# Attention in a two-layer hybrid backbone: transposing all key blocks of two heads, then multiplying both groups' values in one stretch

## The chip, the cores and the metric

The kernel runs on one core of a Trainium2 chip. The metric is device time in microseconds, the median of 3 runs: 1319.07 us (1317.4 to 1320.59). The profile is of one execution of its own.

## The reference, cut to what matters

Two layers, each with three head groups beside each other: a Hyena long convolution, a Mamba-2 scan and windowed attention. 512 latent tokens and 256 context tokens, model width 1024. The change touches attention alone: 8 query heads of 64 channels in 2 groups of 4 that share a key and value head. A latent block of 128 queries sees its own and its neighbouring key blocks and both context blocks; a context block sees the context blocks.

```python
s_loc = jnp.einsum("bnqhgd,bnkhd->bnhgqk", qb, kband).astype(jnp.float32) * scale
s_loc = jnp.where(mask[None, :, None, None], s_loc, -jnp.inf)
s_ctx = jnp.einsum("bnqhgd,bkhd->bnhgqk", qb, kc).astype(jnp.float32) * scale
sink = jnp.broadcast_to(sinks..., (b, nb, ATT_KV_HEADS, ATT_GROUP, WINDOW, 1))
p = jax.nn.softmax(jnp.concatenate([s_loc, s_ctx, sink], -1), axis=-1).astype(v.dtype)
o = (jnp.einsum("bnhgqk,bnkhd->bnqhgd", p[..., :nloc], vband)
     + jnp.einsum("bnhgqk,bkhd->bnqhgd", p[..., nloc:nloc + lc], vc))
```

Everything is float32. The context's own output is needed in layer 0 only.

## The kernel before, in words

`att` (from L577) works through blocks of 128 queries: n = 0 to 3 of the latent tokens and, in layer 0, n = 4 and 5 of the context. A block has nk key blocks of 128: 4, 5, 5, 4 for the latent ones and 2, 2 for the context's. That is 22 key blocks in layer 0 and 18 in layer 1, 40 in all.

For each of the two groups g the block's queries are loaded (L599), split in a high and a low part (`qh`, `ql`), multiplied with the keys (L614, L622, L630, masks L631) and put through a softmax (maxima L632 and L633, exponentials L634 and L636, scaling by the reciprocal sum L645 on ACT for head 3 and L647 on DVE for heads 0 to 2). The probabilities of a group are one tile `pr`, with the queries on the partitions; both groups' tiles are kept in `prs`.

For the product with the values the keys have to be on the partitions. So for each key block i and each group g, four transposes (L654, one a head) fill a bank of PSUM (`wk`, five banks), and a copy brings it to a tile `pt` in SBUF (five buffers of 128 x 512): on DVE (L659), or on ACT (L657) where g is 1 and i is not 0. Then one product a group (L663) adds the block to the accumulator `pv`, which is a bank of `wk` too: group 0 writes partitions 0 to 63, group 1 partitions 64 to 127, 512 columns (four heads) each. A float32 product is two records in the trace. At the end of a block of queries ACT takes the accumulator out (L664) and SP stores it (L665).

The order of the instructions on each engine is not the order of the program text. The tile framework draws it up at compile time: it takes what is ready by its own model of times, in the priority of the program's order, subject to data, free buffers and explicit edges of order; on the chip each engine then keeps that order. This is how the projections of the other head groups (`proj`: L450 for the latent tokens, L452 for the context's) get in among the attention work.

Of the kernel before, what the change touches and what calls it, by code (L numbers as in the profile page):

```python
# [35 lines left out]
# columns of the per-layer parameter block  # L36
C_HCW, C_SCW, C_NW, C_BM = 0, 48, 80, 84
NPAR = 108
# columns of the constant block
K_ID, K_U, K_L, K_ONE = 0, 128, 256, 384  # L40
NCON = 512
# blocks of 128 columns of w_in
# [3 lines left out]
class Net:  # L46
    def __init__(self, ctx, tc, a):
        self.tc, self.nc, self.a = tc, tc.nc, a
        nc = self.nc
        self.one = ctx.enter_context(tc.tile_pool(name="one", bufs=1))  # L50
        self.dr = ctx.enter_context(tc.tile_pool(name="dr", bufs=1, space=DRAM))
        self.ps = ctx.enter_context(tc.tile_pool(name="ps", bufs=1, space=PSUM))
        self.sb = ctx.enter_context(tc.tile_pool(name="sb", bufs=1))
        self.n = 0
        self.kd = {}
        self.th = {}
        self.ph = None
        self.rr = 0

        self.ml = self.tq([P, 4, 768])  # L60
        fw = self.ml[:, 3]
        self.fw = fw
        nc.sync.dma_start(self.ml.rearrange("p a b -> p (a b)")[0:33, 1536:2432], a["mlp1"])
        self.cc = self.one.tile([P, 16], F32, name="cc")
        nc.sync.dma_start(self.cc, a["cc"])
        nc.sync.dma_start(fw[:, 128:392], a["mlp2"])
        self.row = self.one.tile([P, DEPTH, 48], F32, name="row")
        nc.sync.dma_start(self.row, a["row"].partition_broadcast(P))
        self.con = self.one.tile([P, NCON], F32, name="con")
        nc.sync.dma_start(self.con, a["con"])  # L70
        self.ident = self.con[:, K_ID:K_ID + P]
        self.par = self.one.tile([P, DEPTH, NPAR], F32, name="par")
        nc.sync.dma_start(self.par, a["par"].rearrange("l p n -> p l n"))
        self.identb = self.one.tile([P, P], BF16, name="identb")
        nc.vector.tensor_copy(self.identb, self.ident)
        self.maskb = self.one.tile([P, 2, P], BF16, name="maskb")
        mk = self.ip("V", [P, QW])[:, :2 * P]
        nc.sync.dma_start(mk, a["mask"])
        nc.vector.tensor_copy(self.maskb.rearrange("p a b -> p (a b)"), mk)
        self.upper = self.one.tile([P, P], mybir.dt.uint8, name="upper")  # L80
        nc.vector.tensor_copy(self.upper, self.con[:, K_U:K_U + P])
        gc = self.one.tile([P, 512], F32, name="gc")
        self.gc = gc.rearrange("p (q s k) -> p q s k", q=2, s=2)
        self.mhalf = self.one.tile([P, 16], F32, name="mhalf")
        nc.vector.memset(self.mhalf, -0.5)
        for l in range(DEPTH):
            s = self.par[:, l, C_SCW:C_SCW + 32]
            nc.vector.tensor_scalar_mul(s, s, 0.5)
        self.nega = self.one.tile([P, DEPTH, 16], F32, name="nega")
        self.nsink = self.one.tile([P, DEPTH, 8], F32, name="nsink")  # L90
        nc.vector.tensor_scalar_mul(self.nsink, self.row[:, :, 32:40], -1.0)
        self.sc = self.one.tile([P, 8, 32], F32, name="sc")
        nc.vector.memset(self.sc, 0.0)
        # sums over the column groups of the tensor engine
        self.sel = self.one.tile([P, 4], F32, name="sel")
        i4 = self.ident.rearrange("p (q i r) -> p q i r", q=2, i=2)[:, :, :, 0:2]
        nc.vector.tensor_tensor(self.sel.rearrange("p (i r) -> p i r", i=2), i4[:, 0], i4[:, 1], op=ALU.add)

    def vectors(self):
        """The conditioning vectors' silu and the scans' rates."""  # L100
# [23 lines left out]
    def tq(self, shape, dt=F32):  # L124
        """One of the large tiles, whose lives cross phases."""
        t = self.sb.tile([P, 4 * QW], dt, name=self.nm("Q"), tag="Q", bufs=7)
        v = t[:, :int(np.prod(shape[1:]))]
        if len(shape) > 2:
            ax = "abcde"[:len(shape) - 1]
            v = v.rearrange(f"p ({' '.join(ax)}) -> p {' '.join(ax)}", **{x: n for x, n in zip(ax, shape[1:])})  # L130
        return v

    def w(self, tag, shape, dt=F32, bufs=2):
        """A working tile of the present phase."""
        return self.al(self.ph, tag, shape, dt, bufs)

    def ip(self, tag, shape, dt=F32, bufs=2):
        """A working tile of the input projection."""
# [25 lines left out]
    def split(self, src, hi, lo, lo_on=None):  # L164
        """hi + lo = src, both fit float32r; src in PSUM for lo_on="v" alone."""
# [55 lines left out]
    def filter_mlp(self):  # L221
# [8 lines left out]
        def sine(lhsT, rhs, col_b, col_f, out, c0):  # L230
            """sin(freq * (product + bias)) for 256 tokens, reduced in turns."""
# [28 lines left out]
    def filter_tables(self, st):  # L260
        """The cosine and sine tables of one of the streams, and both streams' windows."""
# [16 lines left out]
    def filters(self, l, st):  # L278
        """Spectra of layer l's two filters for one of the streams, over its length."""
# [14 lines left out]
        for o in range(2):  # L294
# [4 lines left out]
            for sd in range(2):  # L299
# [7 lines left out]
                for t in range(NT):  # L307
# [10 lines left out]
                    if t == 0 and sd == 0:  # L318
                        # the direct term is a tap at time 0
# [3 lines left out]
                for q in range(HT):  # L323
                    ps = self.wk()

                    def sums(par):
                        """The sum over the even times, then with the odd ones' added to it."""
# [17 lines left out]
    def modulation(self, l, n, mod, big):  # L345
        """Shift, scale + 1 (as columns) or, for n = 2, gate (without its bias, as rows in DRAM) of both streams."""
# [57 lines left out]
    def norm_in(self, xt, i0, hs, mod, psum=None):  # L404
        """hs: the two [128, 1024] normalised token tiles from tile i0 on."""
# [27 lines left out]
    def proj(self, l, b, xt, both, parts=False):  # L433
# [4 lines left out]
        if parts:  # L438
            # by groups of tokens, as they come from the previous layer
# [15 lines left out]
    def gate(self, pl, pc, out):  # L455
        """2 * silu(u)"""
# [8 lines left out]
    def gate_mul(self, l, b0, j, xt, sp, both):  # L465
        """Block j of a group's output, in DRAM and halved, times 2 * silu(u); returns its tile and a free one."""
# [19 lines left out]
    def ssm_gate(self, l, xt, sp, last):  # L486
        """Also the group RMS norm's factors, to DRAM."""
# [5 lines left out]
        for g in range(2):  # L493
# [7 lines left out]
            # sums over the channels, with the tokens on the partitions  # L501
# [38 lines left out]
    def att_in(self, l, xt, last):  # L540
# [8 lines left out]
        # keys twice, high part over low part  # L549
# [27 lines left out]
    def att(self, l, q, ks, vt, last):  # L577
        """Attention's output takes the place of q, halved, and goes to DRAM."""
        nc = self.nc
        sp = self.dr.tile([4, P, QW], F32, name=self.nm("sp"))  # L580
        for n in list(range(4)) + ([] if last else [4, 5]):
            lat = n < 4
            q0 = n * P if lat else n * P + 1
            # the window's blocks, then the context's; an inner block's own keys come last, in a bank of their own
# [63 lines left out]
            pv = self.wk()  # L648
            for i in range(nk):
                pt = []  # L650
                for g in range(2):
                    ps = self.wk()
                    for h in range(4):
                        nc.tensor.transpose(ps[:, h * P:(h + 1) * P], prs[g][:, h, i * P:(i + 1) * P], self.ident)  # L654
                    t = self.w("pt", [P, 512], bufs=5)
                    if g and i:
                        nc.scalar.activation(t, ps, AF.Copy)  # L657
                    else:
                        nc.vector.tensor_copy(t, ps)  # L659
                    pt.append(t)  # L660
                for g in range(2):
                    r0 = 64 * g
                    nc.tensor.matmul(pv[r0:r0 + 64], lhsT=vt[:, keys[i], r0:r0 + 64], rhs=pt[g], start=i == 0, stop=i == nk - 1)  # L663
# [5 lines left out]
    def ssm_in(self, l, xt, last):  # L669
# [23 lines left out]
        # dt: the 16 columns, high and low parts side by side  # L693
# [18 lines left out]
        # layout (dir, chunk, head)  # L712
# [36 lines left out]
        # X: dt * decay to the end; Z: exp(acs); S: exp(total)  # L749
# [5 lines left out]
        # S2: log(dt) - acs  # L755
# [5 lines left out]
    def ssm(self, l, xT, bt, bc, sc, rd, last):  # L761
        """The scans' output takes the place of B and C, halved, and goes to DRAM."""
# [31 lines left out]
        for c in (0, 1, 2, 3) if last else (4, 5, 0, 1, 2, 3):  # L794
# [6 lines left out]
            # what a token adds to itself: the skip term and the reversed scan's diagonal  # L801
# [20 lines left out]
            # within the chunk: dt * decay, forward above the diagonal and on it, reversed below  # L822
# [25 lines left out]
    def hy_in(self, l, xt, last, b0, fill, x2s):  # L848
# [3 lines left out]
        for j in range(4):  # L852
# [12 lines left out]
            if b0 == B_HV:  # L865
                # folded about the middle: sums and differences, even places first
# [8 lines left out]
    def fold(self, v, f, c0, L):  # L875
        """f's place: v's second half plus and minus its first, reversed."""
# [7 lines left out]
    def hy(self, l, spill, last):  # L884
# [4 lines left out]
        for o in range(2):  # L889
            for st in range(1 if last else 2):  # L890
# [3 lines left out]
                for hf in range(2):  # L894
                    # fold about the middle, then turn: [time, (sum, difference), 256 channels]
# [82 lines left out]
    def out(self, l, cats, rsd, gd, hsrc, done, last):  # L978
# [17 lines left out]
        def weights(k):  # L996
            """Split rows of w_out; as many as fit are kept for the groups to come."""
# [17 lines left out]
        def pieces(i0, i):  # L1015
            """The columns of a token tile as they are finished."""
            return ((0, 512), (512, 256), (768, 256)) if last and i0 + i == 3 else ((0, 512), (512, 512))

        def mul(gi, i0):
# [35 lines left out]
            if final:  # L1055
                # one accumulator after the other: the epilogue of the first ones runs beside the last
# [163 lines left out]
def _constants():  # L1220
# [18 lines left out]
    # all indices of the long transform go even ones first  # L1239
# [42 lines left out]
def _layout(i):  # L1282
    """The inputs, laid out for the loads."""
# [61 lines left out]
```

## Time and profile before

| | |
|---|---|
| median of 3 runs | 1319.07 us |
| span of the profiled execution | 1314.3 us |
| PE, PEld busy | 1248.2 us (95%), 989.3 us (75%) |
| DVE, ACT, POOL busy | 954.1 us (73%), 591.9 us (45%), 130.4 us (10%) |
| DMA | 208.94 MB, mean 159 GB/s |
| L663, the products with the values | 160 records, 60.7 us busy |
| L654, the transposes | 320 records, 48.8 us busy |

The span runs from the first to the last instruction of the program in the one execution that was profiled; its device time is not given apart, and the runs' median lies 4.8 us above its span. Busy times are unions of an engine's records. The records of PE end by a model of its pipeline, so that consecutive ones overlap: the distance of their starts, not their length, is what one costs. PE is the matmuls, PEld the weight loads beside them.

### The profile page before, as it was taken

To read this page: it belongs to the slowest core of one execution; us is meant where nothing else is said; L and a number is where in the kernel's file an instruction comes from. 1 tells how busy PE (TensorE), PEld (TensorE's weight loads), DVE (VectorE), ACT (ScalarE), POOL (GpSimd) and SP (SyncE) were. 2 spreads that over 40 slices of the span, in tenths; PEclk is the share of its full clock that TensorE was granted. 3 is DMA by queue.
4 is the path that set the end of the run, shared out by engine and by line. 5 is a ranking of instruction groups with operands and counts; after the bars stand their busy time and mean duration, and the time that the engine had idled before them with its cause. 6 is when DMAs were issued, how large, how long until landed. Compare 5 with 4: busy or idle time off the path is not lost.

```text
span 1314.3 us, 19207 instructions
## 1 busy us (share of the span) xinstructions
PE 1248.2 (95%) x6942; PEld 989.3 (75%) x6942; DVE 954.1 (73%) x1962; ACT 591.9 (45%) x1151; POOL 130.4 (10%) x117
## 2 busy tenths in 40 slices
PE   5997999999999989999999998999999999899997
PEld 3564887766877777799988777786677687798886
DVE  7889548768556786389846899777677688497676
ACT  5567516646234264333234454455544626343340
POOL 2332010000000000012110232100000000011102
PEclk9999899999998999999989999999999999999999
DMA  6777333112315466854479852441111726855872
GB/s 228 257 269 241 123 112 104 55 33 67 119 59 149 153 182 201 299 184 126 152 236 295 263 191 106 116 114 44 33 57 73 257 71 173 277 170 176 262 251 80
DMA packets 109192, 208.94 MB, mean 159 GB/s; under 512 B 10553, under 2 KB 55033, under 8 KB 109096
## 3 DMA queue, kind: packets, MB, share of 16 engines
q1 hardware_dynamic: 109096, 207.70, 49.7%
q8 instruction: 55, 0.90, 0.3%
q14 instruction: 41, 0.34, 0.1%
HBM read 162.44 MB, written 38.41 MB: 153 GB/s over the span
## 4 chain that ended last, share of the span: by engine, by line
PE 53%; DVE 16%; DMA 11%; issue 10%; ACT 6%; POOL 2%; SPq 1%; POOLq 0%; DVEq 0%; ACTq 0%
PE pl L450 18%; PE pc L452 7%; PE wk L663 4%; PE wk L175 3%; PE wk L177 3%; PE wk L176 3%; PE wk L654 3%; DMA R<-rd 3%; DMA wr<-in_tab_dram 2%; PE wk L622 1%; DMA Q<-in_w_mod_dram 1%; DMA wo<-in_w_out_dram 1%; ACT wh L170 1%; DVE wl L171 1%; DMA wr<-in_fwo_dram 1%
## 5 line engine op out<-in xcount | busy, mean ns | idle before, releaser
L450 PE MATMUL pl<-Q,wh 128*128 128x512 f32 x1168 | 407.4, 403 | 0.0
L450 PEld LDWEIGHTS pl<-Q,wh 128*128 128x128 f32 x1168 | 217.6, 189 | 54.2 <-issue 6.4
L450 PE MATMUL pl<-Q,wl 128*128 128x512 f32 x584 | 232.8, 399 | 0.0
L452 PE MATMUL pc<-Q,wh 128*128 128x256 f32 x704 | 179.4, 291 | 0.3 <-DVE V L463 0.3
L170 ACT ACTIVATE wh<-wr 128x1024 fp32r<-128x1024 f32 x76 | 80.4, 1057 | 183.5 <-PE pc L452 121.3
L452 PEld LDWEIGHTS pc<-Q,wh 128*128 128x128 f32 x704 | 126.8, 193 | 9.4 <-issue 2.7
L450 PEld LDWEIGHTS pl<-Q,wl 128*128 128x128 f32 x584 | 110.3, 189 | 23.6 <-issue 0.8
L171 DVE TENSOR_TENSOR wl<-wr,wh 128x1024 fp32r<-128x1024 f32 x76 | 100.6, 1325 | 35.5 <-ACT wh L170 35.2
L932 POOL TENSOR_TENSOR ta<-ta 128x256 f32<-128x256 f32 x40 | 32.0, 799 | 760.3 <-DVE ta L930 460.0
L452 PE MATMUL pc<-Q,wl 128*128 128x256 f32 x352 | 101.4, 288 | 0.0
L452 PEld LDWEIGHTS pc<-Q,wl 128*128 128x128 f32 x352 | 67.9, 193 | 0.6
L663 PE MATMUL wk<-pt,vt 128*64 128x512 f32 x160 | 60.7, 615 | 0.2 <-DVE pt L659 0.2
L654 PEld LDWEIGHTS wk<-con,pr 128*128 128x128 f32 x320 | 35.8, 141 | 29.8 <-issue 19.9
L632 DVE TENSOR_REDUCE S<-wk 128x1 f32<-128x512 f32 (+1 forms) x80 | 49.4, 631 | 11.7 <-PE wk L631 9.1
L659 DVE COPY pt<-wk 128x512 f32<-128x512 f32 x50 | 33.4, 688 | 31.6 <-PE wk L654 31.3
L634 ACT ACTIVATE pr<-wk,S 128x512 f32<-128x512 f32 (+1 forms) x80 | 51.2, 646 | 7.4 <-DVE S L633 7.2
L833 ACT ACTIVATE R<-R,sc 128x128 f32<-128x128 f32 x120 | 38.6, 391 | 26.3 <-DMA R<-rd 25.2
L654 PE MATMUL wk<-con,pr 128*128 128x128 f32 x320 | 48.8, 279 | 0.0
L170 ACT ACTIVATE wh<-wo 128x1024 fp32r<-128x1024 f32 x30 | 31.6, 1056 | 34.8 <-DMA wo<-in_w_out_dram 13.4
L171 DVE TENSOR_TENSOR wl<-wo,wh 128x1024 fp32r<-128x1024 f32 x30 | 38.7, 1292 | 9.5 <-ACT wh L170 9.5
L175 PE MATMUL wk<-ph,Q 128*128 128x256 f32 x144 | 40.6, 294 | 4.9 <-ACT ph L170 4.9
L170 ACT ACTIVATE yh<-ta 128x512 fp32r<-128x512 f32 x32 | 20.2, 631 | 54.4 <-DVE ta L933 54.2
(393 smaller groups left out, 2929.8 us busy)
## 6 DMA issues: line engine op xcount, KB each, us to landing
wr<-in_w_in_dram SPq DMA_DIRECT2D x76, 512.0 KB, 3.8
Q<-in_w_mod_dram SPq DMA_DIRECT2D x24, 1024.0 KB, 7.3
wo<-in_w_out_dram SPq DMA_DIRECT2D x43, 512.0 KB, 5.5
kd<-k SPq DMA_DIRECT2D x40, 256.0 KB, 2.7
R<-rd SPq DMA_DIRECT2D x20, 512.0 KB, 6.1
kt<-kd SPq DMA_DIRECT2D x40, 256.0 KB, 3.1
sp<-V SPq DMA_DIRECT2D x20, 384.5 KB, 3.9
cs<-sp SPq DMA_DIRECT2D x60, 128.0 KB, 4.1
```

The lines of the kernel that those rows point to most:

```text
L170: nc.scalar.activation(hi, src, AF.Copy)
L171: (nc.gpsimd if lo_on == "p" else nc.vector).tensor_tensor(lo, src, hi.bitcast(F32), op=ALU.subtract)
L175: mm(out, lhsT=lh, rhs=rh, start=start, stop=False, **k)
L176: mm(out, lhsT=lh, rhs=rl, start=False, stop=False, **k)
L177: mm(out, lhsT=ll, rhs=rh, start=False, stop=stop, **k)
L450: nc.tensor.matmul(pl, lhsT=w[:, k * P:(k + 1) * P], rhs=x[:, 0:SEQ], start=s, stop=e)
L452: nc.tensor.matmul(pc[:, 0:CTX], lhsT=w[:, k * P:(k + 1) * P], rhs=x[:, SEQ:SEQ + CTX], start=s, stop=e)
L632: nc.vector.tensor_reduce(m[:, h:h + 1], sa[:, :wa], axis=AX.X, op=ALU.max)
L634: nc.scalar.activation(pr[:, h, :wa], sa[:, :wa], AF.Exp, bias=negm[:, h:h + 1], scale=0.125, accum_out=sums[:, h:h + 1])
L654: nc.tensor.transpose(ps[:, h * P:(h + 1) * P], prs[g][:, h, i * P:(i + 1) * P], self.ident)
L663: nc.tensor.matmul(pv[r0:r0 + 64], lhsT=vt[:, keys[i], r0:r0 + 64], rhs=pt[g], start=i == 0, stop=i == nk - 1)
L833: nc.scalar.activation(R[:, d, h], R[:, d, h], AF.Identity, bias=bias)
```

## The change

In `att` the loop behind the softmax is turned. It now goes over pairs of heads (hp = 0 and 2). For a pair, all nk key blocks are transposed first: one bank of `wk` and one `pt` tile hold a key block of both groups, two heads each (256 columns a group), copied by DVE for even i and by ACT for odd i. Then the products of all key blocks follow, group 0 and group 1 in turn, each of 256 columns, into the pair's half of `pv`. A new helper `after` records an edge of order without a wait between the engines: the first product of each group in a pair (i = 0) comes behind the pair's last transpose in PE's order. `pv` is allocated after the first pair's transposes. The first product of the first pair starts the accumulation of the bank, and the second pair's first does not. Comments and docstrings are also removed throughout the file.

```diff
+    def after(self, later, earlier):
+
+        self.tc.add_manual_dep(later.ins, earlier.ins.name, mybir.DependencyInfo(mybir.DependencyClass.NoSync, mybir.DependencyReason.DATA), reason="order")
...
-            pv = self.wk()
-            for i in range(nk):
-                pt = []
-                for g in range(2):
+            pv = None
+            for hp in range(0, 4, 2):
+                pts = []
+                for i in range(nk):
                     ps = self.wk()
-                    for h in range(4):
-                        nc.tensor.transpose(ps[:, h * P:(h + 1) * P], prs[g][:, h, i * P:(i + 1) * P], self.ident)
-                    t = self.w("pt", [P, 512], bufs=5)
-                    if g and i:
-                        nc.scalar.activation(t, ps, AF.Copy)
+                    for g in range(2):
+                        for h in range(2):
+                            turned = nc.tensor.transpose(ps[:, (2 * g + h) * P:(2 * g + h + 1) * P], prs[g][:, hp + h, i * P:(i + 1) * P], self.ident)
+                    t = self.w("pt", [P, 2, 256], bufs=5)
+                    if i % 2:
+                        nc.scalar.activation(t, ps.rearrange("p (g c) -> p g c", g=2), AF.Copy)
                     else:
-                        nc.vector.tensor_copy(t, ps)
-                    pt.append(t)
-                for g in range(2):
-                    r0 = 64 * g
-                    nc.tensor.matmul(pv[r0:r0 + 64], lhsT=vt[:, keys[i], r0:r0 + 64], rhs=pt[g], start=i == 0, stop=i == nk - 1)
+                        nc.vector.tensor_copy(t, ps.rearrange("p (g c) -> p g c", g=2))
+                    pts.append(t)
+                pv = pv or self.wk()
+                for i in range(nk):
+                    for g in range(2):
+                        r0 = 64 * g
+                        m = nc.tensor.matmul(pv[r0:r0 + 64, hp * P:hp * P + 256], lhsT=vt[:, keys[i], r0:r0 + 64], rhs=pts[i][:, g], start=i == 0 and hp == 0, stop=i == nk - 1, skip_group_check=True)
+                        if i == 0:
+                            self.after(m, turned)
             nc.scalar.activation(q[:, :, q0:q0 + P], pv.rearrange("p (h q) -> p h q", h=4), AF.Copy, scale=0.5)
```

## Rows read from the trace of the kernel before

**Rows 1.** The page, busy time of each engine, and granted clock by slices.
```profile
PE 1248.2 (95%) x6942; PEld 989.3 (75%) x6942; DVE 954.1 (73%) x1962; ACT 591.9 (45%) x1151; POOL 130.4 (10%) x117
PEclk9999899999998999999989999999999999999999
```

**Rows 2.** The page, chain of waits by engine and line, and the products' group.
```profile
PE 53%; DVE 16%; DMA 11%; issue 10%; ACT 6%; POOL 2%; SPq 1%; POOLq 0%; DVEq 0%; ACTq 0%
PE pl L450 18%; PE pc L452 7%; PE wk L663 4%; PE wk L175 3%; PE wk L177 3%; PE wk L176 3%; PE wk L654 3%; DMA R<-rd 3%; DMA wr<-in_tab_dram 2%; PE wk L622 1%; DMA Q<-in_w_mod_dram 1%; DMA wo<-in_w_out_dram 1%; ACT wh L170 1%; DVE wl L171 1%; DMA wr<-in_fwo_dram 1%
...
L663 PE MATMUL wk<-pt,vt 128*64 128x512 f32 x160 | 60.7, 615 | 0.2 <-DVE pt L659 0.2
```

**Rows 3.** Windows: stretch, its length, busy of each engine, clock, DMA share, GB/s.
```profile
190.00:335.00 145.00, 143.51 (x836) 101.02 (x836) 105.72 (x281) 81.36 (x207) 0.80 (x1) 1.00 0.27 82
860.00:985.00 125.00, 123.46 (x722) 90.08 (x722) 86.28 (x198) 65.69 (x159) 1.29 (x1) 1.00 0.22 60
335.00:860.00 525.00, 505.35 (x2972) 424.63 (x2971) 377.80 (x757) 210.53 (x373) 57.07 (x48) 0.99 0.56 174
985.00:1314.00 329.00, 312.09 (x1672) 256.86 (x1670) 245.64 (x463) 130.79 (x223) 25.80 (x25) 0.99 0.55 179
```

**Rows 4.** Timeline of PE, second query block of layer 0: start, length, line.
```profile
237.95 0.27 PE L654 MATMUL wk<-con,pr 128*128 128x128 f32 x1
238.15 1.07 PE L663 MATMUL wk<-pt,vt 128*64 128x512 f32 x2
239.15 1.86 PE L654 MATMUL wk<-con,pr 128*128 128x128 f32 x15
...
242.87 1.94 PE L663 MATMUL wk<-pt,vt 128*64 128x512 f32 x8
244.74 1.64 PE L654 MATMUL wk<-con,pr 128*128 128x128 f32 x13
...
247.78 1.83 PE L663 MATMUL wk<-pt,vt 128*64 128x512 f32 x4
249.54 0.33 PE L614 MATMUL wk<-ks,qh 128*128 128x128 f32 x1
```

**Rows 5.** Timeline of PE, third query block of layer 0.
```profile
269.30 1.08 PE L663 MATMUL wk<-pt,vt 128*64 128x512 f32 x4
270.31 0.55 PE L654 MATMUL wk<-con,pr 128*128 128x128 f32 x3
```

**Rows 6.** Timeline of PE, projections of 512 and 256 columns in turn.
```profile
190.83 0.39 PE L450 MATMUL pl<-Q,wh 128*128 128x512 f32 x1
191.06 0.28 PE L452 MATMUL pc<-Q,wh 128*128 128x256 f32 x1
191.17 0.39 PE L450 MATMUL pl<-Q,wh 128*128 128x512 f32 x1
```

**Rows 7.** Timeline of PEld, weight loads of the products at 242.87.
```profile
242.87 0.20 PEld L663 LDWEIGHTS wk<-pt,vt 128*64 128x64 f32 x4 [0.17 <-DVE V L525]
```

**Rows 8.** All on tile pt: ns min/median/max, first and last start; then waits (us, times).
```profile
L663 PEld LDWEIGHTS wk<-pt,vt x160: 132/136/137, 213.7 to 969.7; 128*64 128x64 f32 x160
L663 PE MATMUL wk<-pt,vt x160: 592/592/644, 213.7 to 970.2; 128*64 128x512 f32 x160
L659 DVE COPY pt<-wk x50: 677/691/692, 209.2 to 968.6; 128x512 f32<-128x512 f32 x50
L657 ACT ACTIVATE pt<-wk x30: 577/597/600, 216.3 to 969.0; 128x512 f32<-128x512 f32 x30
...
  ACT pt L657: 4.2, 8
  DVE pt L659: 3.2, 13
```

**Rows 9.** Timeline of DVE, filler operations in the second query block.
```profile
238.81 1.22 DVE L171 TENSOR_TENSOR wl<-wr,wh 128x1024 fp32r<-128x1024 f32 x1
...
241.74 1.01 DVE L525 SCALAR_TENSOR_TENSOR V<-U,par,V 128x769 f32<-128x769 f32 x1
```

**Rows 10.** The chain of waits in order of time, end of attention in layer 0.
```profile
326.14 5.37 DMA Q<-in_w_mod_dram
```

## The prediction

> **What bounds the kernel now.** I read the page's busy shares first: the reader is to see PE at 95% of the span, DVE at 73% and ACT at 45%, and a granted clock of nine tenths or more in all slices but three, which show eight [rows 1]. The page's chain of waits says where on PE: the value products (L663) and the transposes in front of them (L654) hold 4% and 3% of the chain, some 58 and 40 us [rows 2]. The windows then cut out the two stretches in which attention runs, 190 to 335 us for layer 0 and 860 to 985 us for layer 1: PE is busy 143.5 of 145 and 123.5 of 125 us at a granted clock of 1.00, DVE 73% and 69%, and the DMA share is under 0.3 [rows 3]. Whatever attention doesn't use on PE there, the input projections (L450, L452) of the other head groups fill. So PE is the limit, and PE time taken out of attention should move all that follows.
>
> Where PE time goes within one block of queries shows in the timeline of PE [rows 4]. The records of L663 are halves of a product: 160 records for 40 key blocks of two groups, two passes each. The two groups write 64 output partitions each (128*64 in the form), and they can run beside each other: at 242.87 eight records take 1.87 us to the next matmul's start at 244.74, and at 269.30 four take 1.01 [rows 4, 5]. But at 247.78 four records take 1.76 us, and at 238.15 two alone take 1.00: there one group went without the other, because its transposed copy came later. Twice 1.00 for a key block whose two groups went apart, against 0.86 (1.87 less 1.01) for one more key block with both groups together: that is what the change is about.
>
> **The change part by part.** *Present cost.* In the timeline the 160 records stand in 45 stretches between other matmuls: 19 of two records (1.00 us each, 19.0), 21 of four (1.01 to 1.76, sum 29.2), one of six (1.86) and four of eight (1.87 each, 7.5), the first from 213.7 and the last at 969 to 970 us [rows 8]. Sum 57.6 us; the page's busy time for the line, 60.7 us, agrees, since each stretch's modelled end lies 0.07 us behind the next start (1.07 against 1.00) and 45 times 0.07 is 3.1 [rows 2, 4]. Beside it each stretch costs something at its entry: the transpose ahead of it starts 0.20 us earlier (237.95 to 238.15), where transposes among themselves start every 0.114 us (15 in 1.86 us, the last 0.27 long) [rows 4]. That is 0.09 us a stretch, 4 us in all. Present cost 61.6 us.
>
> *New cost.* Every product is cut in two halves of 256 columns, for heads 0 and 1 and then 2 and 3: 320 records. A copied tile now holds both groups' columns of a key block, so both products come free at once and no group goes alone; and the added order edge puts a half's first product behind its last transpose. Both groups' pass of 512 columns takes 0.43 us when they run together (0.86 over two passes); I take half, 0.215, for 256 columns. 40 key blocks x 2 halves x 2 passes x 0.215 = 34.4 us. A stretch's fixed cost is 0.15 us (1.01 less 0.86) and 0.09 at its entry; with one stretch for each half of ten blocks of queries, 20 x 0.24 = 4.8 us. New cost 39.2 us, a gain of 22.4 us.
>
> That 256 columns cost half is not shown for this form. The nearest rows: the projections alternate 512 and 256 columns, and from 190.83 to 191.06 the first takes 0.23 us, from 191.06 to 191.17 the second 0.115 [rows 6], half within the rounding. From the other side: a weight load of 128x64 lasts 136 ns [rows 8], and if the four loads of a key block and half came one behind the other, they would take 0.544 us where I count 0.43, which gives back 80 x 0.114 = 9.1 us. But four such loads lie within 0.20 us at 242.87 [rows 7], so they run beside each other, and 0.136 lies inside a pass of 0.215. I take the half. A gain below that (a pass under 0.215) I exclude: it would mean columns faster than the type's present rate. The Trainium skill weighs against the cut: TensorEngine Tiling (Array Packing), Instruction Overhead, says that each matmul carries some 60 cycles of overhead. Taken as added time on the 160 records more, two groups side by side, it would be an estimated 80 x 25 ns = 2 us less gain; rows 6 show no such part, since 256 columns there cost no more than half of 512.
>
> *Stretches that break, and copies that come late.* The order edge holds only the first product of a half; the scheduler may still put transposes of the other half or a projection between the later ones. Between 20 stretches and 80 (each key block of each half by itself: 60 x 0.24 = 14.4 us) I take 30, since the copies of all but the last block or two have had the time of the other transposes: minus 2.4 us. Today PE stood 7.4 us in 21 places for a copy of DVE or ACT [rows 8], 0.35 each; with the same wait in 8 of the 20 stretches, minus 2.8 us. Gain on PE 17.2 us.
>
> *Parts that cost nothing.* Transposes: 320 before and after, of the same form. Copies: 80 before and after, of 512 columns; by the new rule (odd key block on ACT) DVE makes 44 and ACT 36 instead of 50 and 30 [rows 8], so 6 x 0.69 = 4 us leave DVE and 6 x 0.60 = 3.6 us come to ACT, which has over a third of both stretches free [rows 3]. If that cover were gone, it would be 3.6 us. The transposes of a half need up to five banks of the five that wk has, and the accumulator is now taken after them; a copy on each of two engines frees a bank every 0.32 us (0.69 and 0.60, alternating), four transposes fill one every 0.46, so they don't run out. The five pt buffers hold a half of five key blocks; the copies of the second half wait for the products of the first, which PE does before it transposes on. The issue of the store (L665) stays behind the eviction, and SP's queue keeps its order. Heads 0 and 1 can be transposed before heads 2 and 3 are scaled, and the probabilities come free earlier as the stage is shorter; what is late next is the next block's softmax chain, which projections cover today.
>
> *What of it reaches the end.* The chain has the whole of L663 on it (4% of 1314 us against the 57.6 counted). Behind the two attention stretches PE is busy 505 of 525 and 312 of 329 us [rows 3], and 11% of the chain is DMA [rows 2]; these start from what attention's stretch leaves finished and should shift with it, with some loss. I take 90%: 15.5 us. The profiled execution's span is 1314.3 us, the median of the runs 1319.07, so some 4.8 us lie around the span: span about 1298.8, time about 1303.5 us. By layers: 18 of the 40 key blocks are layer 1's, so 45% of it.
>
> **The rivals.** *Copies become the bound (slower).* Now the products of a half stand behind all its transposes, and PE runs its queue in order. If the scheduler counts on a copy that on the chip sits behind a filler operation of DVE (1.22 us for L171, 1.01 for L525 [rows 9]), PE stands, and the projections queued behind it too. A copy of 0.69 behind one of 1.22 is up to 1.9 us late; at 20 stretches that is up to 38 us, 16 slower than before. It decides from 22.4/20 = 1.1 us of wait a stretch; with 1.5 the time is 1327. For it: 70% DVE load in these stretches. Against: today's waits are 0.35 us, and the copies of the first blocks of a half now have the time of all its later transposes. The Trainium skill speaks for this rival, in TensorEngine Tiling (Array Packing), PSUM Bottleneck: tiling speeds up TensorE but not the copies out of PSUM, which may become the bottleneck. Against that: in five key blocks' 9.2 us on PE (two halves of 2.3 transposing and 2.3 multiplying) DVE has 6 x 0.69 = 4.1 us of copies. Chance 0.11.
>
> *The gain is eaten behind attention (same).* The attention stretch of layer 0 ends in a wait of 5.4 us for a DMA of the modulation weights [rows 10], and the output projections run by chains of DVE and DMA; if these don't start earlier, time stays near 1318. Against: PE's 96% between the layers. Chance 0.09.
>
> *The stretch doesn't come out as one (smaller gain).* If products follow each copy singly, 80 stretches leave 61.6 - (34.4 + 19.2) = 8 us: about 1311. Rows 4 show that the scheduler does cut in wherever something is ready. Serial weight loads (13.3 us before deductions) end near there too, 1309. Chance 0.22.
>
> **How the numbers follow.** Forecast (a gain of 11 to 22 us) 0.58, smaller gain 0.22, same 0.09, slower 0.11. Runs of this kernel spread by 3 us, so a change under 0.2% (2.6 us) can't be told from none. Faster is the first two, 0.80; same 0.09; slower 0.11. The range reaches to the full 22.4 us and some luck in the new order of the work, 1294, and up to the edge of the same case, 1318, leaving out the slower cases and half of the others above. The forecast's own range is 1297 to 1308.
>
> **What would show it.** Right: L663's successor has 320 records of about 380 ns (592 [rows 8] less 0.215), 20 to 30 stretches in PE's timeline, busy about 41 us in place of 60.7; stretches of 20 records near 2.3 us; PE's waits for pt under 6 us; the second attention stretch begins some 9 us earlier and the rest ends 15 earlier. Wrong: records at a pitch well over 0.215 (halving), many short stretches (order), waits for pt over 20 us (copies), or L663 down by 20 us with an unchanged span, which would show new idle time on PE between 335 and 860 or after 985 us.

## The result, and the profile after

The changed kernel takes 1298.53 us (median of 4 runs, 1296.07 to 1307.45) against 1318.24 us of the kernel before beside it: ratio 0.9859, 95% interval 0.9826 to 0.9892, faster by 18.6 us (14.2 to 22.9). The profiled execution has a span of 1296.6 us in place of 1314.3 and took 1298.41 us. The forecast was 1303.5.

The page's first and second parts, as in [rows 1]:

```profile
PE 1232.7 (95%) x7102; PEld 1000.6 (77%) x7102; DVE 953.0 (74%) x1956; ACT 594.7 (46%) x1157; POOL 129.2 (10%) x117
...
PEclk9999999999999999999999999999999999899999
```

PE is busy for 15.5 us less in a span 17.7 us shorter, with 160 records more; DVE and ACT moved by 1.1 and 2.8 us. The time lies 1.8 us above the span of its own execution. The windows of the products' line alone (L672 is L663's successor), the two layers, with PE's and PEld's busy time:

```profile
0.00:650.00 650.00, 22.08 (x176) 11.67 (x176) 0.98 0.52 158
650.00:1296.00 646.00, 17.75 (x144) 9.84 (x144) 0.98 0.53 164
```

39.8 us of PE, where [rows 2] have 60.7. The timeline of PE, second query block of layer 0, answers to [rows 4]:

```profile
229.85 0.27 PE L661 MATMUL wk<-con,pr 128*128 128x128 f32 x1
...
236.10 2.38 PE L672 MATMUL wk<-pt,vt 128*64 128x256 f32 x20
238.41 2.44 PE L661 MATMUL wk<-con,pr 128*128 128x128 f32 x20
240.78 2.38 PE L672 MATMUL wk<-pt,vt 128*64 128x256 f32 x20
243.09 0.33 PE L618 MATMUL wk<-ks,qh 128*128 128x128 f32 x1
```

Twenty records (five key blocks, two groups, two passes) take 2.31 us to the next matmul, and from the first product on transposes and products alternate in whole halves. From its first transpose at 229.85 the block takes 13.2 us to the next block's scores at 243.09, projections between included. Before, the same way led from 233.29 to 249.54, 16.3 us:

```profile
233.29 0.27 PE L654 MATMUL wk<-con,pr 128*128 128x128 f32 x1
```

All on the tile pt, answers to [rows 8]. The last line says who waited for its copies: the weight loads (PEld), not PE's matmuls.

```profile
L672 PE MATMUL wk<-pt,vt x320: 379/379/431, 212.7 to 946.7; 128*64 128x256 f32 x160
L666 DVE COPY pt<-wk x44: 680/691/692, 211.8 to 944.9; 128x512 f32<-128x512 f32 x44
L664 ACT ACTIVATE pt<-wk x36: 577/598/602, 211.9 to 945.2; 128x512 f32<-128x512 f32 x36
...
  ACT pt L664: 1.9, 7
...
  DVE pt L666: 1.3, 3
...
  PEld wk L672: 3.3, 10
```

The windows, as [rows 3] for stretches shortened by what was gained, show that attention stayed a stretch of nearly full PE at full clock (98% busy, 99% before), and that PE does not stand longer elsewhere (17 us in each of the last two windows, 20 and 17 before):

```profile
190.00:325.00 135.00, 132.04 (x921) 104.76 (x921) 101.81 (x276) 83.10 (x211) 0.00 (x0) 1.00 0.31 90
845.00:960.00 115.00, 113.16 (x788) 92.89 (x786) 84.03 (x196) 66.98 (x161) 1.29 (x1) 1.00 0.26 69
325.00:845.00 520.00, 502.55 (x2949) 422.17 (x2948) 377.10 (x754) 209.82 (x372) 56.39 (x48) 0.98 0.57 174
960.00:1296.60 336.60, 319.83 (x1692) 263.02 (x1690) 248.45 (x465) 131.42 (x224) 25.84 (x25) 0.97 0.57 175
```

The granted clock of the last two windows is 0.98 and 0.97, where the kernel before had 0.99 twice. That is no mark of the change: over the whole span the two kernels' second traces, from one chip, have 0.980 each.

### The profile page after: what moved, and what is told of

Same layout as the page of the kernel before. It is cut to its first block, busy times and chain, and to the rows that moved or that the text cites. A ratio compares the mean times of both kernels' runs of the same rounds, so it can differ in the third digit from the quotient of the medians.

```text
span 1296.6 us, 19528 instructions
## 1 busy us (share of the span) xinstructions
PE 1232.7 (95%) x7102; PEld 1000.6 (77%) x7102; DVE 953.0 (74%) x1956; ACT 594.7 (46%) x1157; POOL 129.2 (10%) x117
## 4 chain that ended last, share of the span: by engine, by line
PE 54%; DVE 15%; DMA 12%; issue 10%; ACT 6%; POOL 2%; SPq 1%; POOLq 0%; DVEq 0%; ACTq 0%
PE pl L454 19%; PE pc L456 7%; PE wk L175 4%; PE wk L176 3%; PE wk L177 3%; PE wk L672 3%; PE wk L661 3%; DMA R<-rd 2%; DMA wr<-in_tab_dram 2%; DMA wr<-in_w_in_dram 2%; PE wk L626 1%; DVE wl L171 1%; ACT wh L170 1%; DMA wo<-in_w_out_dram 1%; DMA Q<-in_w_mod_dram 1%
## 5 line engine op out<-in xcount | busy, mean ns | idle before, releaser
L454 PE MATMUL pl<-Q,wh 128*128 128x512 f32 x1168 | 410.3, 405 | 0.0
L454 PEld LDWEIGHTS pl<-Q,wh 128*128 128x128 f32 x1168 | 219.0, 190 | 54.4 <-issue 7.3
L454 PE MATMUL pl<-Q,wl 128*128 128x512 f32 x584 | 233.8, 400 | 0.0
L456 PE MATMUL pc<-Q,wh 128*128 128x256 f32 x704 | 182.3, 294 | 2.0 <-DVE V L467 1.2
L454 PEld LDWEIGHTS pl<-Q,wl 128*128 128x128 f32 x584 | 111.1, 190 | 23.5 <-issue 0.8
L661 PE MATMUL wk<-con,pr 128*128 128x128 f32 x320 | 45.7, 276 | 0.0
L175 PE MATMUL wk<-ph,Q 128*128 128x256 f32 x144 | 40.9, 297 | 3.1 <-ACT ph L170 3.1
L176 PE MATMUL wk<-plo,Q 128*128 128x256 f32 x144 | 41.6, 293 | 0.6 <-DVE plo L171 0.5
L177 PE MATMUL wk<-ph,Q 128*128 128x256 f32 x144 | 41.1, 290 | 0.0
```

What stands on the lines that cost most here:

```text
L175: mm(out, lhsT=lh, rhs=rh, start=start, stop=False, **k)
L176: mm(out, lhsT=lh, rhs=rl, start=False, stop=False, **k)
L177: mm(out, lhsT=ll, rhs=rh, start=False, stop=stop, **k)
L454: nc.tensor.matmul(pl, lhsT=w[:, k * P:(k + 1) * P], rhs=x[:, 0:SEQ], start=s, stop=e)
L456: nc.tensor.matmul(pc[:, 0:CTX], lhsT=w[:, k * P:(k + 1) * P], rhs=x[:, SEQ:SEQ + CTX], start=s, stop=e)
L661: turned = nc.tensor.transpose(ps[:, (2 * g + h) * P:(2 * g + h + 1) * P], prs[g][:, hp + h, i * P:(i + 1) * P], self.ident)
```

## The experiments

They ran on three chips, where the kernel before took 1323.5 to 1325.8 us (medians); each ratio is to the runs of the kernel before on the same chip, and the comparisons of traces below are across chips unless they say otherwise. Each trace is of one execution. Three numbers are read from every trace. *PE cost* of the products: from the first record of each stretch to the next matmul's start, plus what its entry takes beyond 0.114 us. *Length of attention*: from the first eviction of a layer (ACT takes an accumulator out) to its last, the two layers added. *PE idle*: what PE's busy time leaves of the 160 us from 850 to 1010 us, which hold layer 1's attention and its end.

| kernel | stretches | PE cost, us | length, us | PE idle, us | ratio to before (95%) |
|---|---|---|---|---|---|
| before | 45 | 62.4 | 177.9 | 1.6 | 1 |
| changed, again | 24 | 41.9 | 157.8 | 1.8 | 0.9861 (0.9832 to 0.9890) |
| groups one after the other | 24 | 60.0 | 172.4 | 2.0 | 1.0000 (0.9981 to 1.0019) |
| joint tiles, not collected | 53 | 51.6 | 181.1 | 8.4 | 0.9997 (0.9981 to 1.0012) |
| changed, all copies on DVE | 59 | 51.6 | 172.0 | 2.1 | 0.9940 (0.9916 to 0.9964) |
| changed in layer 0 only | 34 | 51.1 | 167.0 | 1.9 | 0.9944 (0.9924 to 0.9963) |
| changed in layer 1 only | 35 | 53.1 | 168.7 | 2.1 | 0.9932 (0.9910 to 0.9954) |
| joint tiles in layer 0 only | 49 | 55.9 | 179.0 | 1.3 | 0.9968 (0.9948 to 0.9988) |
| joint tiles, projection held | 56 | 56.4 | 182.9 | 18.3 | 1.0128 (1.0103 to 1.0153) |
| joint tiles, copies on DVE | 77 | 58.1 | 187.5 | 8.7 | 1.0050 (1.0026 to 1.0074) |
| changed, copies' engines swapped | 28 | 43.2 | 161.5 | 2.6 | 0.9884 (0.9853 to 0.9915) |

**Groups one after the other.**

```diff
-                for i in range(nk):
-                    for g in range(2):
+                for g in range(2):
+                    for i in range(nk):
```

> The changed kernel, but within a half all products of group 0 are issued first and then all of group 1 (same records, same tiles, same transposes-first). If the gain comes from the two groups' products running beside each other, a stretch of 20 records goes from 2.31 us to about 10 x 0.43 + 0.15 = 4.45 us, PE gets 40 x 0.86 = 34.4 us more work, and at nine tenths of it reaching the end the time is about 1298.5 + 31 = 1329 us, slower than the kernel before. Rival: the gain comes from fewer switches between transposes and products, or from an earlier end of the softmax chain, whatever stands beside what within a stretch: then it stays within 3 us of 1298.5.

The gain is gone: ratio 1.000, 18 us above the changed kernel, with 18.1 us more PE cost. So the gain needs the groups side by side, and the rival (fewer switches, an earlier softmax) is out. The size was off: I expected 11 us slower than before. The timeline of PE shows why:

```profile
242.74 3.73 PE L672 MATMUL wk<-pt,vt 128*64 128x256 f32 x20
246.39 1.86 PE L661 MATMUL wk<-con,pr 128*128 128x128 f32 x15
```

3.65 us to the next matmul and not 4.45. By the records' starts group 0 goes every 0.216 us from its second record on (the first starts at 242.735), and at 244.087 group 1's first starts between group 0's seventh and eighth, though all ten of group 0 stand ahead of it in PE's compiled order (two rows of ten, each 0.216 us apart, tell the groups from each other).

**Joint tiles, not collected.** The new tile, products after each key block's own copy.

```diff
-                pv = pv or self.wk()
-                for i in range(nk):
+                    pv = pv or self.wk()
                     for g in range(2):
...
-                        if i == 0:
-                            self.after(m, turned)
```

> The changed kernel's joint tiles (both groups, two heads) and halves, but each key block's two products follow its own copy as in the kernel before, with no transposes-first and no edge of order. The compiled order has 53 stretches of products in place of 24 (45 before). By the sum, joint tiles give 62.4 - (34.4 + 53 x 0.24) = 15.3 us of PE and the collected stretches 7 us more: time about 1318.2 - 0.9 x 15.3 = 1304.5 us. Rival: the collected stretch is what pays, joint tiles alone don't: 1315 us or more.

PE cost falls by 10.8 us and the time doesn't move: my expectation failed and the rival fits. The timeline of PE at the end of layer 1's attention shows one place where it went:

```profile
972.08 0.65 PE L671 MATMUL wk<-pt,vt 128*64 128x256 f32 x4
972.67 0.87 PE L688 MATMUL wk<-con,V 128*128 128x128 f32 x6
979.25 2.79 PE L688 MATMUL wk<-con,V 128*128 128x128 f32 x12 [5.71 <-DVE V L533]
981.70 0.78 PE L456 MATMUL pc<-Q,wh 128*128 128x256 f32 x2
```

Behind the last products PE stands 5.7 us for a convolution on DVE, with no projection between. The windows of this stretch have PE busy 18.35 of 25 us and a granted clock of 0.86. The last two lines cut it finer: PE stands, the clock falls meanwhile, and when PE goes on it does so for 3.4 us at the lower of the two levels, which costs an estimated 1.7 us:

```profile
960.00:985.00 25.00, 18.35 (x121) 13.65 (x120) 16.82 (x31) 9.92 (x17) 0.00 (x0) 0.86 0.24 75
985.00:1010.00 25.00, 25.00 (x127) 19.23 (x126) 16.12 (x30) 9.08 (x12) 0.00 (x0) 0.93 0.23 64
...
973.50:979.20 5.70, 0.04 (x1) 0.00 (x0) 5.66 (x8) 2.80 (x4) 0.00 (x0) 0.69 0.32 65
979.20:982.60 3.40, 3.35 (x16) 3.38 (x17) 3.16 (x11) 2.12 (x3) 0.00 (x0) 0.51 0.70 284
```

The compiled order had drawn more projections into attention. Between layer 1's first scores and its last product stand 120 records of the projections' line L454 (90 of L450 in the kernel before, 88 in the changed kernel), in layer 0 143 (120 before, 116 changed). The place freed on PE went to them, and attention itself ended no sooner.

**Changed, all copies on DVE.**

```diff
-                    if i % 2:
+                    if i < 0:
```

> The changed kernel with all 80 copies on DVE (0.69 us each) in place of 44 on DVE and 36 on ACT. A half of five copies takes 3.45 us against 2.3 us of transposing, so products must wait or be spread: the compiled order has 59 stretches. If PE's occupancy is what counts: 8.4 us more fixed cost on PE, time about 1298.5 + 0.9 x 8.4 = 1306 us. Rival, that the copies out of PSUM are close to being the bound: PE stands for pt by over 15 us in all, and the time is 1312 us or more. Third: DVE had slack and the spread order hides it, within 3 us of 1298.5.

8 us faster than before and some 10 slower than the changed kernel, 4 slower than the sum said. Over the changed kernel's the PE cost is up by 9.7 us, which is what the time lost. The rival did not come: the weight loads wait 3.1 us for pt, where it asked for over 15. PE cost is the joint variant's, 51.6 us, to the tenth, and the time differs by 7.6 us (0.9940 against 0.9997). The same stretch at the end of layer 1 as above shows where: PE does not stand, and the joint variant's 5.7 us of wait and 1.7 us of lower clock make 7.4. (The 0.93 behind it stands in both.)

```profile
960.00:985.00 25.00, 24.65 (x160) 19.12 (x159) 19.81 (x35) 9.53 (x13) 0.00 (x0) 1.00 0.23 75
985.00:1010.00 25.00, 24.98 (x126) 18.70 (x125) 17.23 (x39) 7.86 (x11) 0.00 (x0) 0.93 0.22 64
```

**Changed in one layer only.** The new code under `if l == 0:` or `if l == 1:`, the old one in the other layer.

> The change in layer 0 alone; layer 1 as before. The trace of the changed kernel shows 11.2 us less of PE in layer 0's stretches and 9.3 in layer 1's. If both reach the end alike at nine tenths: 1318.2 - 10 = 1308 us. Rival: layer 1's share is given back behind attention, where the changed kernel waits longer for the modulation weights: then layer 0 alone has nearly all of the gain, 1302 us or less.

> The change in layer 1 alone; layer 0 as before. Layer 1's 9.3 us less of PE at nine tenths: ratio 0.9936 (8.4 us less). If the two layers add up to the whole (0.9859, layer 0 alone measured 0.9944): ratio 0.991 to 0.992 (11 us less). Rival, that layer 1's share is given back behind attention at the modulation weights: 0.997 or above.

Layer 0 alone brings 7.4 us of its 11.2 us of PE cost, layer 1 alone 9.0 of 9.3 (each with 3 us either way), so that neither rival came. Their sum, 16.4, agrees with the whole, 18.4. In the layer-0-only trace the projections come 10.2 us earlier across layer 0's attention (from 3.9 late to 6.3 early against the second trace of the kernel before, which is from another chip) and are 3.0 early by layer 1. In the layer-1-only trace 9.0 us early becomes 11.8 and falls back to 8.7 at the modulation weights.

**The two kernels again.**

> The kernel before, unchanged, so that there is a trace of it from the chip on which the variants run. Its products take 57.6 us in 45 stretches as in the first trace; its time is within 3 us of the kernel before's on this chip.

> The changed kernel, unchanged, beside the variants and with more runs. Ratio to the kernel before 0.986 as in the first comparison, between 0.983 and 0.989; 38.2 us in 24 stretches.

Both as expected. By the projections' starts in their traces, both from one chip, the changed kernel gains 10.2 us in layer 0's attention and 10.4 in layer 1's, and gives back 3 to 4 us at layer 1's modulation weights, where PE's one wait is 2.7 us (0.7 in three before). The chain of waits has the transfer in the changed kernel, then in the kernel before: it starts 16.8 us earlier, about as much as PE's work around it, and takes 1.5 us longer. Why it does is open. Behind the wait the granted clock is low for some 3 us more, an estimated 1.7 us (last line, the changed kernel):

```profile
PE wk L363 <- DMA Q<-in_w_mod_dram: 2.7, 1, 2.7
...
1019.95 8.57 DMA Q<-in_w_mod_dram
...
1036.70 7.06 DMA Q<-in_w_mod_dram
...
1028.50:1033.00 4.50, 4.43 (x16) 2.82 (x17) 1.65 (x7) 1.46 (x3) 0.00 (x0) 0.62 0.76 208
```

**Joint tiles in layer 0 only.** The joint variant's code under `if l == 0:`.

> Joint tiles without collected stretches in layer 0 alone; layer 1 as before. In the trace of the joint variant layer 0's projections came some 7 us earlier and layer 1's attention then ended 3 us later than before, behind one wait of 5.7 us of PE for a convolution on DVE and two drops of the clock. If that end of layer 1 is what ate the joint tiles' gain: ratio 0.994 to 0.996 (6.5 us less of PE in layer 0). Rival, that joint tiles without collected stretches bring nothing in either layer: 0.998 to 1.002.

0.9968 lies between: 4.2 us of layer 0's 6.5 arrive, so, if the layers add up, layer 1 turned its part into a loss of some 3.8 us (4.2 less 0.4, each with 2 to 3 us either way). That fits the end of layer 1 seen above: 4.3 us less PE cost there, against 7.4 us of wait and lower clock.

**Joint tiles, projection held.**

```diff
+                if hold and s:
+                    self.after(m, hold)
...
-            pl, pc = self.proj(l, B_XS + j, xt, True)
+            pl, pc = self.proj(l, B_XS + j, xt, True, hold=self.lastpv if last and j == 2 else None)
```

> The joint variant with one edge of order more: in layer 1 the projection of the scan's third input block may not start on PE before attention's last product. In the joint variant all four of these projections were drawn into attention, so that at its end PE had only transposes that wait for convolutions on DVE (5.7 us in one wait, and a clock of 0.86 between 960 and 985 us). If that end ate its gain, the wait goes under 2 us and the ratio comes to 0.991 to 0.994 (56 stretches: 62.4 - 34.4 - 56 x 0.24 = 14.5 us of PE by the sum, 10 by the joint variant's trace). Rival, that products which are not collected bring nothing whatever stands at the end: 0.998 to 1.002.

17 us slower, neither case. The wait at the end is gone, but inside attention PE ran dry, as the groups of PE from 910 to 985 us show (last columns: idle before, and what ended it):

```profile
L663 PE MATMUL wk<-con,pr 128*128 128x128 f32 x112 | 21.3, 319 | 10.1 <-DVE pr L653 10.0
L673 PE MATMUL wk<-pt,vt 128*64 128x256 f32 x112 | 18.0, 426 | 2.4 <-DVE pt L668 2.3
```

Of the projections' line 24 records are left between the first scores and the last product, in place of 120. So they were needed there: the chain of softmax, transposes and products has gaps that they fill. At 24 records a projection, five inside leave the end without filler, and one inside leaves the gaps without it.

**Joint tiles, copies on DVE.** Both edits at once.

> The joint variant with all copies on DVE: 77 stretches in the compiled order, and again four blocks' transposes at the end of layer 1's attention with no projection among them. By PE alone: 62.4 - (34.4 + 77 x 0.24) = 9.5 us less, ratio 0.9935. If the end of layer 1 decides, a wait of 4 to 6 us stands there again and the ratio is 0.997 to 1.001. Third, if the joint variant lost because its copies on ACT stood ahead of the convolutions: no wait, 0.9935.

0.5% slower than before, beyond the second case. The wait of 5.7 us at the end of layer 1 is there again, so ACT's queue is not its cause. PE cost is 4.3 us less than before, but PE stands 7.1 us more from 850 to 1010.

**Changed, copies' engines swapped.**

```diff
-                    if i % 2:
+                    if i % 2 == 0:
```

> The changed kernel with the copies' engines swapped: even key blocks on ACT, odd ones on DVE, so ACT makes 44 and DVE 36. 28 stretches in the compiled order in place of 24, 1 us of PE. If the length of attention's own chain decides and neither copy engine limits it: ratio 0.985 to 0.989, like the changed kernel. Rival, that DVE, the busier engine, is what the blocks wait for: 0.983 or less, and a version better than both.

As expected: no better than the change, so DVE's load is not what the blocks wait for. No version tried beats the changed kernel.

## Why the prediction was right, point by point

*Groups side by side.* The sum's main term held: both groups take 0.432 us for a key block and half where 0.43 was forecast, records of 379 ns where 380 was, stretches of twenty records 2.31 us. Undoing the side-by-side alone gives the whole gain back. So it is needed; that it is not enough, the joint tiles show.

*Half the columns at half the cost.* Shown by the same stretches: a pair of passes of 256 columns takes 0.216 us, as one group's pass alone does in the serial variant. The Trainium skill's overhead for each matmul (TensorEngine Tiling (Array Packing), Instruction Overhead), taken as added time, is not to be seen here: 160 records more added nothing.

*Stretches and waits.* There are 24 stretches, not 30, and each costs some 0.30 us beside its passes (7.3 us in all) where 0.24 was taken. The deduction of 2.8 us for waits rests on a misreading: the 7.4 us of [rows 8] are idle time of the weight loads, and PE's own matmuls waited 0.2 us for a copy, as the lines of the kernel before on who waited say:

```profile
  PEld wk L663: 7.2, 20
...
  PE wk L663: 0.2, 1
```

In the changed kernel the weight loads wait 3.3 us and the matmuls not at all. PE cost fell by 20.5 us, where I had taken 17.2 after the two deductions.

*The time.* It came out 5 us below the forecast. Of that 3 us is the gain (18.6 for 15.5), which follows from the two deductions; the rest is that the kernel before ran 0.8 us faster beside the change, and the spread of the medians. I also took the 4.8 us between the profiled span and the median for time around the span. It is not: each run lies 1.8 us above its own span, so the execution profiled before was a fast one. This left the forecast of the time alone, but made that of the span 3 us too low (1298.8; with 1.8 it would be 1301.7; measured 1296.6).

*What reaches the end.* 18.6 of 20.5, nine tenths as forecast. With 14.2 to 22.9 us as the interval the share itself is not measured, so that its hitting is in part luck. One place of the loss is seen in layer 1, at the modulation weights: a longer wait, and the lower clock behind it.

*The step whose condition was left out.* I argued that PE is the limit in attention and that PE time taken out of it moves all that follows. That came out where PE had other work in its place. In seven rows of the table the time follows PE cost to within 4 us: 20.5 us less PE cost and 18 us less time for the change, 19 and 15 with the engines swapped, 11 and 8 with all copies on DVE, 11 and 7 in layer 0 only, 9 and 9 in layer 1 only, 6.5 and 4 for joint tiles in layer 0, 2.4 and 0 for serial groups. In the three others it doesn't: 10.8 less PE cost and no less time for the joint tiles, 4.3 less and 7 us more time for these with copies on DVE, 6 less and 17 more for the held projection. They are the only rows in which PE stands for more than 3 us from 850 to 1010 us (windows of the kernel before, the joint tiles, the held projection, the copies on DVE):

```profile
850.00:1010.00 160.00, 158.39 (x894) 117.09 (x892) 111.97 (x239) 78.66 (x174) 3.88 (x3) 1.00 0.24 68
850.00:1010.00 160.00, 151.63 (x952) 118.00 (x951) 106.98 (x234) 78.19 (x174) 2.60 (x2) 0.97 0.24 63
850.00:1010.00 160.00, 141.66 (x865) 107.51 (x864) 99.87 (x221) 72.72 (x166) 3.88 (x3) 0.95 0.21 59
850.00:1010.00 160.00, 151.28 (x925) 114.45 (x924) 118.42 (x251) 69.85 (x159) 3.87 (x3) 0.99 0.24 65
```

They stand there 6.8, 16.7 and 7.1 us more than the kernel before. With that added to PE cost the sum meets the time to within 4 us again for two of them, and to 6 for the held projection, where the granted clock was 0.95 besides. So the argument lacked a condition: PE time taken out pays as long as PE has other work to put there and still has some at the stage's end. The joint tiles and all copies on DVE show it at equal PE cost, 51.6 us: the first stand at the end of layer 1 and gain nothing, the second don't and gain 8 us. The joint tiles in layer 0 alone, with layer 1 as before, gain 4.

The length of attention goes with the time in many rows, but it is not the cause. It misses the serial groups (5.5 us shorter, the same time), the joint tiles in layer 0 (1 longer, 4 faster) and the held projection (5 longer, 17 slower), and it counts the projections that the compiled order puts in between: in both layers 263 records for the joint tiles, 204 for the changed kernel, 210 before. A projection drawn in lengthens attention and shortens what follows. What collecting the products did, beyond the 9.7 us of PE cost that fewer stretches save, is in these counts: it left the projections where they were, while products behind each single copy drew 53 more in. Why the framework orders them so is open, and so are the 2 to 4 us by which the time falls short of PE cost in most rows, about what the intervals leave either way.

*The rivals.* Copies as the bound did not come: the weight loads wait 3.3 us for them in ten places, PE's matmuls not at all. The Trainium skill's rule that spoke for it (TensorEngine Tiling (Array Packing), PSUM Bottleneck) is not borne out by either trace: with DVE alone copying, the weight loads wait 3.1 us too. What breaks then is the compiled order, into 59 stretches, and 10 us of the gain go. A stretch in pieces did not come either. Its price, 1311 us, is near what 59 pieces cost with all copies on DVE (0.9940, 1310 us beside 1318.24); the joint tiles' 53 pieces gained nothing, for the reason above.

## What to carry to other kernels

Two products that each use half of the array's output columns cost as one here (0.216 us a pass of 256 columns, for one group alone and for both), if their operands come free together and they are issued in turn; a tile that holds both operands sees to the first. Where another stage's work fills the gaps, count not only what the busy engine saves but also where that filler goes: filler that is drawn forward is missing at the stage's end. Collecting the products behind all transposes left it in place here; half the saving in PE time without that (10.8 of 20.5 us) was worth nothing, because PE then stood.

## What the runs showed of the hardware

Products on the two column halves are not held to PE's compiled order: with group 1's ten records (five products) behind group 0's ten in that order, group 1's first starts 1.35 us after group 0's first, the last four of group 0 passing beside the first four of group 1, so that twenty records take 3.65 us and not 4.45. To this extent it does not hold that an engine keeps the compiled order on the chip, or that PE runs its queue in order, as was said ahead of the result.
